# A hybrid decoder layer in fp32: the gate product as seven half-size products, after the whole output projection

## The chip, the cores and the metric

The kernel runs on one core of a Trainium2 chip. The metric is the device time of one execution in microseconds (us), as the median of repeated runs. The core has five engines that take instructions in order and wait for each other by semaphores: TensorE (PE) for matmuls, VectorE (DVE), ScalarE (ACT), GpSimd (POOL), and SyncE (SP), which issues the transfers (DMA) between the chip's memory and the core's on-chip memory SBUF. Matmul results land in PSUM, which has eight banks here; one bank holds 128x512 fp32 numbers.

## What is computed

One decoder layer on 2048 tokens of width 1024, all in fp32. Tokens are normalised and projected; 512 columns go through a state-space layer, 512 through causal differential attention with 4 heads. What comes after that is what the change touches:

```python
x = x + jnp.concatenate([y_s, y_a], axis=-1) @ w_out[i]
gate = jax.nn.sigmoid((x @ ple_w_gate[i]).astype(jnp.float32)).astype(x.dtype)
x = x + gate * (p[i] @ ple_w_proj[i])
```

`w_out` and `ple_w_gate` are 1024x1024, `ple_w_proj` is 256x1024. The last line has the PLE product, `p[i] @ ple_w_proj[i]`.

## The kernel before, in words

**Precision.** An fp32 operand is split into a high part, a cast to fp32r, and a low part, the difference of the number and its high part. A product is made in three passes (`passes`): high by high, high by low, low by high. ACT casts; DVE or POOL subtracts. Every matmul of the last phase multiplies a 128x128 weight block with 128x256 of the transposed activations, 256 tokens. So tokens come in eight units of 256, and a 1024x1024 product of one unit is 8 blocks of k by 8 of m by 3 passes, 192 matmuls; the half-size ones (512 of k, the output projection's second half) are 96, and PLE's are 48.

**Stages.** First the input projection and the state-space layer, whose result `y_s` gives the first half of the output projection, summed with the input `x` into `xp_scr` in the chip's memory beside the attention (`half`). Then attention, head by head, unit by unit; in the last head units come in the order 7, 6, ... 0. A query tile of 128 tokens ends in a chain of dependent steps: score transposes on PE (L1085), a copy on ACT (L1087), value matmuls into `po` (L1089), a square with its sum on ACT (L1092), three tiny steps on POOL (L1096 to L1098), DVE (L1099), one more transpose on PE (L1100), ACT's copy to `yo` (L1101), and a store to `yt_scr`, from which the projection loads its `yin`.

**The last phase (L1113 on).** `out_proj(i)` loads a unit's `xp_scr` as `x1` and its attention result (`load_y`: `yin`, `yh` cast on ACT at L911, `yl` difference on POOL at L912), makes four groups of 24 matmuls (`project`, L921), and DVE adds each group from PSUM to `x1` (L1138). The first three units (`EOP`) go into the pool `ps_f`, one PSUM bank that exists beside attention's (`pmf`); the others use `ps3`, the seven banks that attention leaves (`pm`). `split` casts `x1` (ACT, L1146) and subtracts (POOL, L1147) for the gate product. Per unit and block m of 128 columns PE then makes 24 gate matmuls (L1176) and 6 PLE matmuls (L1180) into one bank; ACT takes tanh (L1183), DVE does two fused steps (L1184, L1185), and the result is stored (L1188). The projection of a unit two ahead is laid behind each unit's gate. `resident` loads a weight 128 rows at a time into a buffer `yin`, casts it on ACT (L898) and subtracts on DVE (L899). It makes the second half of `w_out` (`wob`) at a fixed step of the last head, and in the last phase all of `w_gate` and `w_proj`.

**Order.** The program is written in one order of statements with priorities, and a scheduler lays the instructions of each engine in a fixed order before the run. It puts projection matmuls between the steps of the last attention units ("fillers" below). A pool of buffers can be opened on memory of another only when that one is done as a whole.

## Time and profile before

| | before |
|---|---|
| median of three runs | 1479.39 us (1478.57 to 1480.09) |
| the profiled execution | 1482.44 us, of which the span from first to last instruction is 1480.7 us |
| PE busy | 1414.4 us, 96% |
| DVE, ACT, POOL busy | 968.3, 747.7, 470.5 us |
| mean granted PE clock | 0.983 of full speed |

The profile is one execution; its times count from the first instruction. Busy is the time in which an engine executes. A row of the timeline gives start, duration, engine, line, and in square brackets how long the engine was idle ahead of it and what ended that. The chain of waits is followed back from the last instruction, at each step to what released it.

### The profile page before, as it was taken

The page shows a single profiled execution, that of the slowest core. Times are in us where ns is not written, and L with a number is a line of the kernel's source. Part 1 is how long each engine was busy: PE and PEld are TensorE (multiplying, and loading weights), DVE is VectorE, ACT ScalarE, POOL GpSimd, SP SyncE. Part 2 cuts the span into 40 slices and gives each one's busy share as a digit, 9 for nine tenths or more (in the row PEclk, how much of TensorE's full clock was granted, in tenths as well). Part 3 has the DMA queues.
Part 4 walks back from the last instruction along what each step waited for, and adds up shares of the span by engine and source line. Part 5 has one row for each costly group of instructions (what it writes and reads, how often), then busy time and mean ns, then how long its engine had stood idle before and what let it go on. Part 6 is the DMA issues. An engine that isn't in the chain of part 4 may idle for free. (4 is left out here: it accounts for less than half of the span.)

```text
span 1480.7 us, 27620 instructions
## 1 busy us (share of the span) xinstructions
PE 1414.4 (96%) x9794; PEld 1303.3 (88%) x9794; DVE 968.3 (65%) x2477; ACT 747.7 (50%) x1663; POOL 470.5 (32%) x654
## 2 busy tenths in 40 slices
PE   7899899999999999999899999999999899999998
PEld 7898798788798878887799999999889889999998
DVE  8578788799898956773777766777876253222222
ACT  8443345546644545552667677777686441111111
POOL 5632410043011410440354345455334512222110
PEclk9999999999999999999999999999999999999999
DMA  7439656546755387557753544544442243111101
GB/s 242 143 113 287 187 187 194 182 140 195 242 165 177 103 233 208 129 156 213 232 147 116 172 132 127 167 136 129 122 172 93 86 143 115 60 52 55 65 27 39
DMA packets 217971, 217.78 MB, mean 147 GB/s; under 512 B 62552, under 2 KB 169192, under 8 KB 216808
## 3 DMA queue, kind: packets, MB, share of 16 engines
q1 hardware_dynamic: 217832, 216.01, 47.9%
q8 instruction: 77, 1.26, 0.4%
q14 instruction: 62, 0.51, 0.1%
HBM read 145.90 MB, written 78.43 MB: 151 GB/s over the span
## 5 line engine op out<-in xcount | busy, mean ns | idle before, releaser
L822 PE MATMUL pmm<-wl,xh 128*128 128x512 f32 x512 | 202.8, 398 | 2.2 <-DVE wl L281 2.1
L822 PE MATMUL pmm<-wh,xl 128*128 128x512 f32 x512 | 202.2, 397 | 0.0
L822 PE MATMUL pmm<-wh,xh 128*128 128x512 f32 x512 | 198.3, 398 | 3.8 <-ACT wh L280 2.5
L1053 PE MATMUL pss<-ks,qd 128*128 128x512 f32 (+3 forms) x640 | 187.5, 390 | 9.8 <-DVE st L1055 4.1
L1064 ACT ACTIVATE s<-s,st 128x1024 f32<-128x1024 f32 (+4 forms) x192 | 171.5, 897 | 36.5 <-DVE st L1055 32.3
L1089 PE MATMUL po<-vt,wt 128*128 128x128 f32 x1088 | 151.1, 277 | 2.3 <-ACT yo L1101 1.5
L1089 PEld LDWEIGHTS po<-vt,wt 128*128 128x128 f32 x1088 | 142.0, 193 | 11.0 <-ACT yo L1101 2.8
L1176 PE MATMUL pm<-xh,wgl 128*128 128x256 f32 x512 | 143.3, 283 | 0.2 <-DVE wgl L899 0.2
L1176 PE MATMUL pm<-xl,wgh 128*128 128x256 f32 x512 | 142.6, 282 | 0.0
L1176 PE MATMUL pm<-xh,wgh 128*128 128x256 f32 x512 | 137.7, 283 | 2.1 <-ACT wgh L898 2.1
L1055 DVE CUSTOM_DVE_ANT_0 s<-pss,mk,st 128x512 f32<-128x512 f32 (+2 forms) x192 | 121.4, 652 | 26.5 <-PE pss L1053 25.1
L776 PE MATMUL pmm<-xh,wl 128*128 128x256 f32 x448 | 127.5, 288 | 2.9 <-DVE wl L281 2.9
L776 PE MATMUL pmm<-xl,wh 128*128 128x256 f32 x448 | 127.4, 288 | 0.0
L776 PE MATMUL pmm<-xh,wh 128*128 128x256 f32 x448 | 124.1, 291 | 3.2 <-DVE stg L786 2.6
L1184 DVE SCALAR_TENSOR_TENSOR th<-th,pm 128x256 f32<-128x256 f32 x64 | 26.8, 420 | 150.3 <-ACT th L1183 150.2
L1053 PEld LDWEIGHTS pss<-ks,qd 128*128 128x128 f32 x640 | 102.4, 193 | 20.9 <-DVE st L1055 8.7
L822 PEld LDWEIGHTS pmm<-wh,xh 128*128 128x128 f32 x512 | 97.2, 191 | 24.8 <-ACT wh L280 4.4
L822 PEld LDWEIGHTS pmm<-wl,xh 128*128 128x128 f32 x512 | 97.6, 191 | 21.4 <-DVE wl L281 3.0
L822 PEld LDWEIGHTS pmm<-wh,xl 128*128 128x128 f32 x512 | 97.7, 191 | 18.4
L1183 ACT ACTIVATE th<-pm 128x256 f32<-128x256 f32 x64 | 24.3, 384 | 169.6 <-PE pm L1180 168.7
L921 PE MATMUL pmf<-yh,woh 128*128 128x256 f32 x352 | 103.3, 294 | 4.8 <-DVE x L1138 3.5
L1147 POOL TENSOR_TENSOR xl<-x,xh 128x512 fp32r<-128x512 f32 x32 | 41.3, 1309 | 199.2 <-ACT xh L1146 104.7
(361 smaller groups left out, 4037.6 us busy)
## 6 DMA issues: line engine op xcount, KB each, us to landing
wraw<-in_w_in_dram SPq DMA_DIRECT2D x96, 256.0 KB
xraw<-in_x_t_dram SPq DMA_DIRECT2D x40, 256.0 KB
tab<-tab_scr SPq DMA_DIRECT2D x64, 136.0 KB
qd<-qh_scr SPq DMA_DIRECT2D x64, 128.0 KB
qd<-ql_scr SPq DMA_DIRECT2D x64, 128.0 KB
xr<-in_x_t_dram SPq DMA_DIRECT2D x32, 256.0 KB
yin<-yt_scr SPq DMA_DIRECT2D x16, 512.0 KB
xp_scr<-xp SPq DMA_DIRECT2D x32, 256.0 KB
```

Source lines behind the costliest of these rows:

```text
L776: T.matmul(pm, lhsT=w[b_][:, cb * 128:cb * 128 + 128], rhs=xt[a_][:, k, :], start=(k == 0 and n == 0), stop=(k == 7 and n == 2))
L822: T.matmul(pm, lhsT=xt[a_][:, k, j * 128:j * 128 + 128], rhs=w[b_], start=(k == 0 and n == 0), stop=(k == 7 and n == 2))
L921: T.matmul(pm[:, e, :], lhsT=w[k][b_][:, ms], rhs=y[a_][:, k, :], start=(k == 0 and n == 0), stop=(k == 3 and n == 2))
L1053: T.matmul(pss[:, :cl], lhsT=qd[:, e, m, tq], rhs=ks[m][:, c0:c0 + cl], start=e == 0, stop=e == 1)
L1055: V.tensor_tensor_reduce(sr[m][pi][:, o:o + cl], pss[:, :cl], mk[:, end - cl:end], scale=1.0, scalar=3.4e38 if ci == 0 else st[:, 2 * ci - ...
L1064: A.activation(sr[m][pi][:, :cl], sr[m][pi][:, :cl], AF.Exp, bias=st[:, ci + m:ci + m + 1], scale=-1.0, accum_out=st[:, 12 + 2 * pi + m:13 ...
L1089: T.matmul(po[:, 0:128], lhsT=wt[:, k, :], rhs=vt[:, kg + k, :], start=kg + k == 0, stop=kg + k == len(blocks_) - 1)
L1147: G.tensor_tensor(xl, x1[:, n0:n0 + 2], xh.bitcast(F32), op=ALU.subtract)
L1176: T.matmul(pm[:, 0], lhsT=wg[0][k][b_][:, ms], rhs=xc[k // 2][a_][:, k % 2], start=(k == 0 and n == 0), stop=(k == 7 and n == 2))
L1183: A.activation(th, pm[:, 0], AF.Tanh, scale=0.5)
L1184: V.scalar_tensor_tensor(th, th, 1.0, pm[:, 1], op0=ALU.add, op1=ALU.mult)
```

## The change

**The gate product by pairs.** Two units, a and b, are taken together, and the 2x2 blocks are halves of k (of `x1`, 512 each), halves of m, and the two units. Seven products of half size (4 blocks of k, 4 of m, 3 passes: 48 matmuls each, 256 tokens wide) take the place of eight. Their activation operands are halves of `x1` or sums of such halves (`s1`, `s2`, `s3`), made on DVE, then cast on ACT and subtracted on POOL (`operands`). Their weights are four quarters of `w_gate` and sums of these. The products are joined in PSUM-to-SBUF sums on DVE (`plus`), tanh and the two fused steps come after that, 512 columns wide.

**The phases.** All eight units go through the output projection first. The finished `x1` of six units is stored to `x1_scr` and loaded again for the gate; the last two stay. Two units, not three, are laid into attention's end. The projection's buffers and banks are then closed (`wo_ctx.close()`), and the gate opens its own: four banks for gate products, four for PLE.

**The weights.** The 56 tiles (7 products, 4 blocks of k, high and low; 128x512) are made in four steps, one behind each of the fourth to seventh units. A step first copies one element of the preceding unit's `x1` into both raw buffers (POOL), so that the loads (SP) come no earlier. The loads of `w_out` take four different slots.

```diff
-EOP = 3
+EOP = 2
...
-                    for k in range(4):
-                        wob[1](k)
+                    for k, slot in enumerate(("yin", "yl", "yin", "yh")):
+                        wob[1](k, slot)
...
+            def gate_w():
+                c1, c2 = slice(0, 512), slice(512, 1024)
+                def made(n, src, eng):
+                    hi, lo = wg[n][k]
+                    A.copy(hi, src)
+                    eng.tensor_tensor(lo, src, hi.bitcast(F32), op=ALU.subtract)
...
+                for k in range(4):
+                    r1, r2 = (pr3.tile([128, D], F32, name="wgr") for _ in range(2))
+                    for r_, k_ in ((r1, k), (r2, k + 4)):
+                        G.tensor_copy(r_[:, 0:1], last[0])
+                        nc.sync.dma_start(r_, w_gate[0][k_ * 128:k_ * 128 + 128, :])
+                    made(1, r1[:, c1], G)
+                    t1 = diff(r1[:, c2], r1[:, c1])
+                    made(5, t1, V)
+                    t2 = diff(r2[:, c2], t1)
+                    made(6, t2, V)
+                    yield
+                    made(2, r2[:, c1], G)
+                    made(4, diff(r2[:, c1], t2), V)
+                    made(7, diff(r2[:, c2], r1[:, c2]), V)
+                    made(3, r2[:, c2], G)
+                    yield
...
+            for t, i in enumerate(order):
+                x1 = px3.tile([128, 8, 256], F32, name="x1")
+                nc.sync.dma_start(x1, xp_scr[i])
+                y = load_y(pa3, i, 512, 2)
+                for n0 in range(0, 8, 2):
+                    pm = (ps_f if t < EOP else ps3).tile([128, 2, 256], F32, name="pmf" if t < EOP else "pm3")
+                    project(pm, wob[0], y, n0)
+                    V.tensor_tensor(x1[:, n0:n0 + 2], x1[:, n0:n0 + 2], pm, op=ALU.add)
+                if t < 6:
+                    nc.sync.dma_start(x1_scr[i], x1)
+                else:
+                    kept.append(x1)
+                if 3 <= t < 7:
+                    next(gw)
+                    next(gw)
+                last[0] = x1[:, 7, 0:1]
+        wo_ctx.close()
...
+        def product(n, x_):
+            banks = [ps_g.tile([128, 2, 256], F32, name="pg3") for _ in range(2)]
+            for mp in range(2):
+                for e in range(2):
+                    m = mp * 2 + e
+                    for k in range(4):
+                        for q, (a_, b_) in enumerate(passes):
+                            T.matmul(banks[mp][:, e], lhsT=wg[n][k][b_][:, m * 128:m * 128 + 128], rhs=x_[a_][:, k],
+                                     start=k == 0 and q == 0, stop=k == 3 and q == 2)
+            return banks
...
+            bk = step(1)
+            for mp in range(2):
+                A.copy(p1[:, mp * 2:mp * 2 + 2], bk[mp])
+            th = logits(step(2), p1)
+            plus(u2, step(6), p1)
+            u3 = pb3.tile([128, 4, 256], F32, name="p1")
+            plus(u3, step(7), u2)
+            gated(ia, 0, th, xa, ple(pa_, 0))
+            bk = step(5)
+            th = logits(bk, u3)
+            plus(u2, bk, u2)
+            gated(ib, 1, th, xb, ple(pb_, 1))
+            bk = step(3)
+            if j < 6:
+                nxt = [load_x1(order[j + 2])]
+            th = logits(bk, u2)
+            gated(ia, 1, th, xa, ple(pa_, 1))
...
```

Three places show what the change moves. Line numbers of the changed kernel are two higher up to the last phase. The first is PE at the end of attention, around the last transpose of `ya` (L1100 before, L1102 after). Before:

```order
L921 MATMUL pmf<-yl,woh_14304 128x256
L921 MATMUL pmf<-yh,woh_14306 128x256
L921 MATMUL pmf<-yh,wol_14307 128x256
L921 MATMUL pmf<-yl,woh_14306 128x256
L1100 MATMUL po<-ident,ya 128x128
L921 MATMUL pmf<-yh,woh_14300 128x256
L921 MATMUL pmf<-yh,wol_14301 128x256
L921 MATMUL pmf<-yl,woh_14300 128x256
L921 MATMUL pmf<-yh,woh_14302 128x256
L921 MATMUL pmf<-yh,wol_14303 128x256
```

After:

```order
L923 MATMUL pmf<-yl,woh_14312 128x256
L923 MATMUL pmf<-yh,woh_14314 128x256
L923 MATMUL pmf<-yh,wol_14315 128x256
L923 MATMUL pmf<-yl,woh_14314 128x256
L1102 MATMUL po<-ident,ya 128x128 x2
L1091 MATMUL po<-vt,wt 128x128 x5
L1102 MATMUL po<-ident,ya 128x128 x2
L1091 MATMUL po<-vt,wt 128x128 x2
L1102 MATMUL po<-ident,ya 128x128
L923 MATMUL pm_14922<-yh,woh_14308 128x256
L923 MATMUL pm_14922<-yh,wol_14309 128x256
```

Before, projection matmuls stand on both sides of the last transpose; after, the last transposes and value matmuls (L1091) follow each other, and the rest of the projection begins, in `pm`, behind the last of them.

The second is POOL from the end of attention on. `st` are the small steps of a query tile, `xl` and `pl` the low parts of the gate's and PLE's operands, `yl` that of the projection's, `wgr` the raw weight, `wg` its tiles. Before:

```order
L1147 TENSOR_TENSOR xl_14919<-x_14654,xh_14918 128x512
L1147 TENSOR_TENSOR xl_14923<-x_14654,xh_14922 128x512
L1147 TENSOR_TENSOR xl_14927<-x_14654,xh_14926 128x512
L1147 TENSOR_TENSOR xl_14931<-x_14654,xh_14930 128x512
L1147 TENSOR_TENSOR xl_15225<-x_14806,xh_15224 128x512
L1096 TENSOR_SCALAR st<-st 128x1 x2
L1147 TENSOR_TENSOR xl_15229<-x_14806,xh_15228 128x512
L1157 TENSOR_TENSOR pl<-pi,ph 128x512
L1097 TENSOR_TENSOR st<-st 128x1 x2
L1098 TENSOR_TENSOR st<-st,negh 128x1 x2
L912 TENSOR_TENSOR yl<-yin,yh 128x1024
```

After:

```order
L1098 TENSOR_SCALAR st<-st 128x1
L1099 TENSOR_TENSOR st<-st 128x1
L1100 TENSOR_TENSOR st<-st,negh 128x1
L1152 COPY wgr<-x_14914 128x1 x2
L914 TENSOR_TENSOR yl<-yin,yh 128x1024
L1142 TENSOR_TENSOR wg_14618<-wgr,wg_14617 128x512
L1142 TENSOR_TENSOR wg_14626<-wgr,wg_14625 128x512
L1142 TENSOR_TENSOR wg_14634<-wgr,wg_14633 128x512
L914 TENSOR_TENSOR yl<-yin,yh 128x1024
L1152 COPY wgr<-x_15027 128x1 x2
L1142 TENSOR_TENSOR wg_14620<-wgr,wg_14619 128x512
```

The low parts of the gate's operands are gone from attention's end, and behind it the two copies, the projection's `yl` and three low parts of a weight step take turns.

The third is PE where the gate begins. `oph` and `opl` are the high and low parts of an operand, `wg` the weight tiles, `pg` the banks. Before:

```order
L921 MATMUL pmf<-yh,wol_14307 128x256
L921 MATMUL pmf<-yl,woh_14306 128x256
L1176 MATMUL pm_14940<-xh_14918,wgh_14640 128x256
L1176 MATMUL pm_14975<-xh_14918,wgh_14640 128x256
L1176 MATMUL pm_15011<-xh_14918,wgh_14640 128x256
L1176 MATMUL pm_15046<-xh_14918,wgh_14640 128x256
L1176 MATMUL pm_15082<-xh_14918,wgh_14640 128x256
L1176 MATMUL pm_15117<-xh_14918,wgh_14640 128x256
L1176 MATMUL pm_15153<-xh_14918,wgh_14640 128x256
L1176 MATMUL pm_14940<-xh_14918,wgl_14641 128x256
L1176 MATMUL pm_14940<-xl_14919,wgh_14640 128x256
```

After:

```order
L923 MATMUL pm_15676<-yh,woh_14314 128x256
L923 MATMUL pm_15676<-yh,wol_14315 128x256
L923 MATMUL pm_15676<-yl,woh_14314 128x256
L1250 MATMUL pg_15764<-oph,wg_14617 128x256
L1250 MATMUL pg_15764<-oph,wg_14618 128x256
L1250 MATMUL pg_15765<-oph,wg_14617 128x256
L1250 MATMUL pg_15765<-oph,wg_14618 128x256
L1250 MATMUL pg_15824<-oph,wg_14625 128x256
L1250 MATMUL pg_15824<-oph,wg_14626 128x256
L1250 MATMUL pg_15825<-oph,wg_14625 128x256
L1250 MATMUL pg_15825<-oph,wg_14626 128x256
L1250 MATMUL pg_15764<-opl,wg_14617 128x256
```

Before, seven banks are begun with the first high parts before the first low weight is needed; after, eight matmuls need only high operands, and the ninth needs `opl`.

## Rows read from the trace of the kernel before

**Rows 1.** The page: busy time by engine; the last chain by line.

```profile
PE 1414.4 (96%) x9794; PEld 1303.3 (88%) x9794; DVE 968.3 (65%) x2477; ACT 747.7 (50%) x1663; POOL 470.5 (32%) x654
...
PE pm L1176 11%; PE pm L921 4%; PE pm L1180 3%; PE pmf L921 2%; DMA yin<-in_ple_w_gate_dram 1%; PE po L1089 1%; DVE wgl L899 0%; ACT wgh L898 0%; PE ptw L1085 0%; DMA yin<-in_ple_w_proj_dram 0%; DVE x L1138 0%; DMA yt_scr<-yo 0%; PE pss L1053 0%; DVE wpl L899 0%; ACT wph L898 0%
```

**Rows 2.** The chain of waits: start in us, duration in us, what ran.

```profile
1186.44 3.29 DMA yin<-in_ple_w_gate_dram
...
1192.09 5.56 DMA yin<-in_ple_w_gate_dram
...
1248.59 11.52 PE pm L921 x96
1260.11 2.83 PE pm L1176 x24
1262.94 0.71 PE pm L1180 x6
...
1288.51 11.52 PE pm L921 x96
```

**Rows 3.** Windows: length, busy time by engine (instructions), PE clock, DMA share, GB/s.

```profile
1192.00:1198.00 6.00, 4.54 (x35) 4.26 (x35) 1.29 (x2) 1.37 (x2) 0.00 (x0) 1.00 0.84 251
1198.00:1204.00 6.00, 5.22 (x31) 5.23 (x32) 2.45 (x2) 2.10 (x3) 0.00 (x0) 0.72 0.37 122
1250.00:1300.00 50.00, 50.00 (x423) 50.00 (x422) 12.81 (x24) 8.44 (x17) 11.88 (x9) 1.00 0.26 90
```

**Rows 4.** PE's timeline: the last head, attention's end, the first gate matmuls, the end.

```profile
1076.64 0.90 PE L1085 MATMUL ptw<-ident,s 128*128 128x128 f32 x3 [4.55 <-ACT wt L1087]
...
1159.63 0.38 PE L1085 MATMUL ptw<-ident,s 128*128 128x128 f32 x2
...
1178.22 0.71 PE L1089 MATMUL po<-vt,wt 128*128 128x128 f32 x4 [0.35 <-ACT yo L1101]
...
1182.59 0.39 PE L921 MATMUL pmf<-yh,woh 128*128 128x256 f32 x1 [0.67 <-DVE x L1138]
...
1198.78 1.67 PE L1176 MATMUL pm<-xh,wgh 128*128 128x256 f32 x7 [2.12 <-ACT wgh L898]
...
1476.37 0.28 PE L1180 MATMUL pm<-pl,wph 128*128 128x256 f32 x1
```

**Rows 5.** ACT's timeline: the last `w_out` cast of the wait, and attention's end.

```profile
1071.17 1.05 ACT L898 CAST woh<-yin 128x1024 fp32r<-128x1024 f32 x1 [2.29 <-DMA yin<-in_w_out_dram]
...
1178.96 0.28 ACT L1092 ACTIVATE ya<-po 128x128 f32<-128x128 f32 x1 [0.54 <-PE po L1089]
...
1181.95 0.37 ACT L1101 ACTIVATE yo<-po,subw 128x128 f32<-128x128 f32 x1 [2.62 <-PE po L1100]
```

**Rows 6.** POOL's timeline: the last `yl`, and an `xl`.

```profile
1169.84 2.41 POOL L912 TENSOR_TENSOR yl<-yin,yh 128x1024 fp32r<-128x1024 f32 x1 [1.36 <-DMA pi<-in_p_t_dram]
...
1187.13 3.27 POOL L912 TENSOR_TENSOR yl<-yin,yh 128x1024 fp32r<-128x1024 f32 x1 [6.58 <-ACT yh L911]
1217.96 2.74 POOL L1147 TENSOR_TENSOR xl<-x,xh 128x512 fp32r<-128x512 f32 x2 [27.55 <-PE pm L1176]
```

**Rows 7.** DVE's timeline: attention's end, gate weights, the first fused steps, the end.

```profile
1180.59 0.35 DVE L1099 SCALAR_TENSOR_TENSOR ya<-po,st,zg 128x128 f32<-128x128 f32 x1 [2.22 <-POOL st L1098]
...
1186.93 1.22 DVE L899 TENSOR_TENSOR wgl<-yin,wgh 128x1024 fp32r<-128x1024 f32 x1
...
1218.54 2.44 DVE L1185 SCALAR_TENSOR_TENSOR x<-th,x 128x256 f32<-128x256 f32 x2
...
1477.56 0.42 DVE L1185 SCALAR_TENSOR_TENSOR x<-th,x 128x256 f32<-128x256 f32 x1
```

**Rows 8.** Groups by line from 1150 us on: busy us, mean ns, idle before.

```profile
L1138 DVE TENSOR_TENSOR x<-x,pm 128x512 f32<-128x512 f32 x20 | 13.7, 687 | 36.5 <-PE pm L921 36.5
L1157 POOL TENSOR_TENSOR pl<-pi,ph 128x512 fp32r<-128x512 f32 x8 | 10.5, 1313 | 1.3 <-ACT ph L1156 1.3
L1146 ACT CAST xh<-x 128x512 fp32r<-128x512 f32 x32 | 19.5, 622 | 28.4 <-issue 14.3 <-DVE x L1138 12.1 <-PE pm L1176 1.6
```

More of the change, by code (lines that the diff above doesn't have):

```diff
@@ new lines, in hymba_kernel, with step @@
+        xa, xb = kept
+        order = order[6:] + order[:6]
+        for j in range(0, 8, 2):
+            ia, ib = order[j], order[j + 1]
+            if j == 0:
+                ops = operands(xa, xb)
+                ready = [next(ops), next(ops)]
+                ple_w()
+            pa_, pb_ = load_p(ia, 0), load_p(ib, 1)
+            p1, u2 = (pb3.tile([128, 4, 256], F32, name=n) for n in ("p1", "u2"))
+            def step(n):
+                bk = product(n, ready.pop(0))
+                nx = next(ops, None)
+                if nx is not None:
+                    ready.append(nx)
+                return bk
+            bk = step(1)
+            for mp in range(2):
+                A.copy(p1[:, mp * 2:mp * 2 + 2], bk[mp])
[13 more added lines that the diff above has]
+            gated(ia, 1, th, xa, ple(pa_, 1))
+            if j < 6:
+                nxt.append(load_x1(order[j + 3]))
+                ops = operands(*nxt)
+                ready.append(next(ops))
+            lb = ple(pb_, 0) if j == 6 else None
+            bk = step(4)
+            th = logits(bk, u3)
+            gated(ib, 0, th, xb, lb or ple(pb_, 0))
+            if j < 6:
+                xa, xb = nxt
```

162 lines of the change are left out of this document (92 added, 70 removed).

## The prediction

> **What bounds the kernel now.** The busy shares come first: TensorE (PE) is busy for 1414.4 of 1480.7 us, and the chain that ended last is mostly its matmuls [rows 1]. The chain of waits shows where that holds. From 1216 us it is an unbroken row of matmuls with one period of 39.92 us (1248.59 to 1288.51): 96 of the output projection in 11.52 us, 0.1200 us each, and eight times 24 of the gate and 6 of the PLE product, 28.40 us for 240, 0.1183 us each [rows 2]. In the window 1250 to 1300 PE is busy for 50.00 of 50 us, VectorE (DVE) for 12.81, ScalarE (ACT) for 8.44, GpSimd (POOL) for 11.88 [rows 3]. A matmul taken out there is time taken out.
>
> Three places are not of that kind. From 1182 to 1212 us the chain goes through the loads, casts and differences of the gate weights [rows 2]. From the matmul at 1182.59 to PE's end at 1476.65 [rows 4] lie 294.1 us; 504 matmuls of the output projection (24 and five units) by 0.1200 and 1920 others by 0.1183 are 287.6, so the late weights cost 6.5 us. At 1076 us PE idles 4.55 us, because ACT first waits 2.29 us for a load of `w_out` and then works off the exponentials queued behind that cast [rows 4, 5]. And while the last attention units run, PE is kept busy by output-projection matmuls laid between their dependent steps [rows 4].
>
> The measure: the profiled execution took 1482.44 us, its span is 1480.7, the median of the runs is 1479.39. I sum on the span and take the difference from the median. The runs agree within 1.5 us, so 0.2%, or 3 us, is about what a measurement here can tell from no change.
>
> **Matmuls.** 1536 gate matmuls become 7 products of 48 for each of 4 pairs, 1344; PLE's 384 and the output projection's 768 stay. The form is the same, 128x128 by 128x256. 192 by 0.1183 is 22.7 us, all on the path by [rows 3]. The phase behind the projection is 1728 matmuls, 204.4 us.
>
> **The weight loads of the projection.** The four loads of `w_out` now have slots of their own, where two waited for a buffer; the 2.29 us wait of ACT goes, and with it about 2 of PE's 4.55 us. Bounds 0 and 4.
>
> **Attention's end.** Only two units fill it, so 192 matmuls, not 264, stand ahead of the last transpose of `ya`, and 184 of them, not 136, ahead of the last score transposes, which ran at 1159.63 [rows 4] (the counts are those of the order of PE's instructions). These come at 1159.6 + 48 x 0.120 - 2 = 1163.4. Behind them three links run bare: value matmuls, ACT's square, three POOL steps, DVE, transpose, ACT's copy. The last link of before takes from 1178.22 to 1182.32, 4.1 us with 24 fillers in it; its unfilled steps (0.7 of matmuls, 1178.96 to 1180.94, transpose and copy 0.7) make 3.4 [rows 4, 5, 7]. 1163.4 + 0.4 + 3 x 3.4 = T, 1174. The projection's other banks are opened only when attention's are closed, so its 576 remaining matmuls start at T. Before was at 1182.6 with 264 fillers done; 72 fewer by 0.120 is 8.6, so the two are equal: the bare idle eats what the missing fillers give. Bounds of T: 1171, if the first link is ready as the transposes end, and 1179, if POOL's `yl` of 2.41 us [rows 6] stands in front of two links. Then the clock: after PE's idle 2.12 us at 1198.78 the granted clock is 0.72 in the mean of 6 us, that is at its lower level for some 3.4 of them: 1.7 us lost [rows 3, 4]. I charge 1.7 at T. The last 576 matmuls take 69.1 us.
>
> **The held-back weight steps.** Each of the four copies one element of the previous unit's `x1` into both raw buffers (POOL), loads 1 MB, and makes 14 tiles with 7 casts on ACT, 3 differences on POOL, 4 differences and 4 low parts on DVE. In POOL's order the copies stand right behind the `yl` of a later unit, and the next `yl` right behind the step's three differences; in ACT's order the `yh` cast stands behind the casts. So a step holds the next unit's operand. One period, by [rows 2, 5, 6, 8]: copies 0.4; two loads of 512 KB, 3.29 us alone and 5.56 with another in flight, together about 6.1; behind the second, casts (0.62) and DVE operations of 512 columns (half of 1.22) in turn, about 4.5; `yh` 1.05; `yl` 2.41. That is 14.5, plus 1.5 for the 1 MB store of `x1` ahead in the queue: 16 us. A unit takes 11.5. The first copy comes when the third unit's `x1` is summed, T + 12.2; the last unit's `yl` is three periods later, and its 11.5 us of matmuls follow. Against 69.1 that is a wait of 3P - 45.4: 2.6 us at P = 16, none below 15.1, 8.6 at 18. The copies themselves wait for a DVE sum; behind the first stands only the fifth unit's `yl`, needed 11 us later, and on SyncE (SP) behind the loads the sixth and seventh units' `yin`, with 20 us to spare: nothing. In exchange the late gate weights of before, 6.5 us, are gone: no gate load is waited for by a gate matmul, unless step four ends after the last unit, and by the same sum it ends 3 us earlier.
>
> **The passage to the gate.** The first operand's cast waits for the projection's last matmul, since their buffers overlay; then cast 1.05, difference 2.41 to 3.27 [rows 6], while PE has only 8 matmuls, 0.9 us, that need the high part alone. Idle 2.6 to 3.7: I take 3.4, and 1.7 for the clock as above.
>
> **The gate phase.** A pair has 432 matmuls, 51.1 us. DVE: five operand sums of 1.22, 14 sums from PSUM of 0.69, 8 times 0.69 and 0.85 (the steps of 0.42 now two in one), 28 us. POOL: 7 x 2.41 and 2 x 1.31, 20. ACT: 7 x 1.05 and 12 x 0.62, 15 [rows 5 to 8]. All lie beside PE; if that cover were gone, POOL's would cost first. The x1 that goes out and comes back, 12 MB, runs in windows whose DMA share was 0.26 [rows 3].
>
> **The end.** Before, PE's end to the span's end is 4.05 us: tanh, two DVE steps of which the last ends at 1477.98, and the store of 128 KB, 2.7 us [rows 4, 7]. Now a sum of 0.69, then 512-wide tanh 0.62, 0.69, 0.85, and a store of 256 KB, taken at the same 2.7 since it comes in one piece: 5.7 with gaps. Bounds 5 and 7.
>
> **Sum.** 1174 + 1.7 + 69.1 + 2.6 + 3.4 + 1.7 + 204.4 + 5.7 = 1462.6, 18.1 under 1480.7; from the median 1461.3. I say 1462.
>
> **A rule against the change.** Beside each other the two engines slow down in the trace: POOL's `yl` takes 3.27 us where a DVE difference runs beside it, 2.41 elsewhere, and two of DVE's L1185 take 2.44 beside POOL's `xl`, where one alone takes 0.42 [rows 6, 7]. The Trainium skill, "GPSIMD Engine Reference", section "1. Specifications", says that POOL shares SBUF interfaces with VectorE and contends with its instructions that have two SBUF inputs. The changed kernel puts just such differences on both engines in every step; by that rule every step would be a long one. The trace agrees where both ran.
>
> **Rivals,** their times taken from the median too. (A) The steps fit and the links are short: T 1171, no weight wait, 2.6 at the passage: 1455. For it: the period's parts overlap more than I let them. Against: 1.05 and 2.41 in a row on two engines are measured. (B) Contention as in the paragraph above: POOL's operations 0.86 longer; in a step `yl` and three differences of half the size give 0.9 + 1.3, P 18.2, the wait 9.2, and the passage 0.5 longer: 1468. For it speaks [rows 6]; against, DVE works only 5 us in a step. (C) The pair boundary: the second half's `x1` is 1 MB and comes through the queue of the output stores; then two sums of 1.22, cast 1.05, `opl` 2.41 to 3.27, some 6 to 7 us, while products 1 and 2 cover 11.4. If the load takes 8 instead of 4, the third product is late by 3 us and the clock falls for 1.7, three times: 14 us, 1475. Against: the windows' DMA share [rows 3]. (D) Slower: the step's period is the bound. Loads of 1 MB stand in one queue with the 1 MB store, the next `x1` and the next `y`; if all four are worked off ahead of a step, 3.5 MB at 251 GB/s [rows 3] is 14 us in place of 7.6, P 22.4, the wait 21.8, and PE's clock falls at each of three waits, 5 more: 1485. It decides from P = 21 on. For it: one queue carries everything. Against: stores of a finished unit can run while the step computes. (E) That the gate isn't made with fewer matmuls: the order has 1344, so nothing.
>
> **How the numbers follow.** My sum 0.60; A 0.13; B 0.10; C 0.10; D 0.07. The forecast's own bounds (T, P from 15 to 18, the end) are 1456 to 1468. The range 1454 to 1475 takes in A and B and leaves out D, most of C and a little above and below. Faster by over 0.2% is all of the sum, A and B and half of C, 0.88; D gives slower 0.06; the rest, 0.06, lies within.
>
> **What would show it.** Right: PE without gaps from the passage to the end, 51 us a pair; a bare stretch of some 10 us with three waits for DVE before the first `pm` of L923; the waits of L923 on POOL's `yl` small and only for the last one or two units; one gap of 3 us at the first `opl`. Wrong: L923 waiting for `yl` at every unit from the fifth (D, or B if POOL's operations are over 3 us), L1250 waiting for `opl` inside each pair (C), or PE waiting at T for more than 12 us.

## The result, and the profile after

The changed kernel takes 1462.24 us (median of 4 runs, 1459.01 to 1467.58), the kernel before 1479.74 beside it. The ratio is 0.9883, with a 95% interval of 0.9851 to 0.9916: by that ratio it is faster by 17.3 us. The forecast was 1462. The profiled execution took 1463.21 us, its span is 1461.5.

Two profiles differ by some us in code that is the same in both. The same PE instruction, the 349th of the `ptw` matmuls, starts here in the trace of before and in that of after (PE's timeline: start, duration, line, operation; in brackets the idle time ahead of it and what ended it):

```profile
1011.42 0.55 PE L1085 MATMUL ptw<-ident,s 128*128 128x128 f32 x3 [0.29 <-ACT wt L1087]
```

```profile
1008.20 0.55 PE L1087 MATMUL ptw<-ident,s 128*128 128x128 f32 x3 [0.29 <-ACT wt L1089]
...
1159.66 0.38 PE L1087 MATMUL ptw<-ident,s 128*128 128x128 f32 x2
...
1162.28 1.38 PE L1091 MATMUL po<-vt,wt 128*128 128x128 f32 x10 [1.06 <-ACT yo L1103]
1165.99 1.00 PE L1102 MATMUL po<-ident,ya 128*128 128x128 f32 x2 [2.33 <-DVE ya L1101]
...
1170.21 0.47 PE L1102 MATMUL po<-ident,ya 128*128 128x128 f32 x1 [2.06 <-DVE ya L1101]
1171.14 0.58 PE L923 MATMUL pm<-yh,woh 128*128 128x256 f32 x1 [0.46 <-ACT yo L1103]
...
1245.96 0.71 PE L1250 MATMUL pg<-oph,wg 128*128 128x256 f32 x4 [3.35 <-ACT oph L1223]
```

Up to that row PE has the same instructions in the same order in both, so I take the 3.2 us between 1011.42 and 1008.20 for no effect of the change. From here on I count from this **mark**. Before, the mark is 469.3 us from the span's end, after 453.3. The other rows of the second fence are the last score transposes (1159.66), three of the waits of attention's bare end, T (1171.14) and the first gate matmul (1245.96); the rows of before that answer to them are in [rows 4]. T is the first `pm` matmul of the projection, with 576 to go; stretches from the last transposes are counted from the second of the two.

By the page, PE's busy time fell by 22.5 us, from 1414.4 [rows 1] to this (busy time; then the chain by engine):

```profile
PE 1391.9 (95%) x9602; PEld 1278.8 (87%) x9602; DVE 1064.7 (73%) x2515; ACT 766.1 (52%) x1657; POOL 522.6 (36%) x670
...
PE 44%; DVE 19%; DMA 15%; POOL 7%; ACT 6%; issue 6%; SPq 3%; DVEq 0%; ACTq 0%; POOLq 0%
```

The chain is less PE than one would think: DVE and DMA have a large share of it since it runs through the weight steps, which PE does not wait for. That is seen in the windows (columns as in [rows 3]):

```profile
1150.00:1175.00 25.00, 19.03 (x130) 17.25 (x130) 6.13 (x17) 9.17 (x32) 9.29 (x24) 0.81 0.51 178
...
1200.00:1225.00 25.00, 25.00 (x211) 25.00 (x210) 19.70 (x20) 8.68 (x14) 14.32 (x11) 1.00 0.71 274
1246.00:1252.00 6.00, 5.96 (x35) 5.75 (x36) 5.96 (x3) 0.58 (x2) 4.45 (x2) 0.72 0.00 0
1300.00:1350.00 50.00, 50.00 (x419) 50.00 (x418) 32.04 (x35) 14.15 (x19) 21.00 (x9) 1.00 0.26 83
```

From 1200 to 1225, in the middle of the weight steps, PE is busy for 25.00 of 25 us. In the gate phase, 1300 to 1350, it is busy for 50.00 of 50, with DVE at 32.04, ACT at 14.15 and POOL at 21.00; before, the same length had DVE at 12.81 and POOL at 11.88 [rows 3]. The granted clock falls in two of these windows, to a mean of 0.81 around T and of 0.72 around the first gate matmul.

### The profile page after: what moved, and what is told of

The parts are those of the page before. It is cut to its first block, busy times and chain, and to the rows that moved or that the text cites. A ratio compares the mean times of both kernels' runs of the same rounds, so it can differ in the third digit from the quotient of the medians.

```text
span 1461.5 us, 27371 instructions
## 1 busy us (share of the span) xinstructions
PE 1391.9 (95%) x9602; PEld 1278.8 (87%) x9602; DVE 1064.7 (73%) x2515; ACT 766.1 (52%) x1657; POOL 522.6 (36%) x670
## 4 chain that ended last, share of the span: by engine, by line
PE 44%; DVE 19%; DMA 15%; POOL 7%; ACT 6%; issue 6%; SPq 3%; DVEq 0%; ACTq 0%; POOLq 0%
PE pg L1250 11%; PE po L1091 7%; PE pss L1055 6%; PE pmf L923 6%; PE pmm L823 4%; PE pl L1266 3%; PE ptw L1087 3%; DMA wraw<-in_w_in_dram 2%; POOL qst L845 2%; DMA tab_scr<-tx 2%; PE pss L706 1%; DMA wgr<-in_ple_w_gate_dram 1%; ACT s L1066 1%; DVE wgt L1146 1%; DVE zz L643 1%
## 5 line engine op out<-in xcount | busy, mean ns | idle before, releaser
L1250 PE MATMUL pg<-oph,wg 128*128 128x256 f32 x896 | 163.3, 285 | 3.3 <-ACT oph L1223 3.3
L1091 PE MATMUL po<-vt,wt 128*128 128x128 f32 x1088 | 151.5, 277 | 2.1 <-ACT yo L1103 1.8
L1091 PEld LDWEIGHTS po<-vt,wt 128*128 128x128 f32 x1088 | 142.7, 193 | 10.2 <-ACT yo L1103 3.3
L1250 PEld LDWEIGHTS pg<-oph,wg 128*128 128x128 f32 x896 | 140.8, 194 | 3.5 <-ACT oph L1223 3.5
L1250 PE MATMUL pg<-opl,wg 128*128 128x256 f32 x448 | 127.1, 285 | 0.0
L1057 DVE CUSTOM_DVE_ANT_0 s<-pss,mk 128x512 f32<-128x512 f32 (+3 forms) x128 | 78.2, 629 | 39.3 <-PE pss L1055 35.3
L1089 ACT COPY wt<-ptw 128x512 f32<-128x512 f32 (+3 forms) x160 | 80.8, 517 | 37.5 <-PE ptw L1087 32.3
L595 POOL TENSOR_TENSOR U<-U,rl 128x256 f32<-128x256 f32 x32 | 30.4, 951 | 186.4 <-DMA U<-ug_scr 145.9
L923 PE MATMUL pmf<-yh,woh 128*128 128x256 f32 x320 | 93.6, 293 | 1.7 <-ACT xp L979 1.4
```

The source lines that it names most:

```text
L595: UE.tensor_tensor(U, U, rl, op=ALU.mult)
L923: T.matmul(pm[:, e, :], lhsT=w[k][b_][:, ms], rhs=y[a_][:, k, :], start=(k == 0 and n == 0), stop=(k == 3 and n == 2))
L1057: V.tensor_tensor_reduce(sr[m][pi][:, o:o + cl], pss[:, :cl], mk[:, end - cl:end], scale=1.0, scalar=3.4e38 if ci == 0 else st[:, 2 * ci - ...
L1089: A.copy(wt[:, :nk], ptw[:, :nk])
L1091: T.matmul(po[:, 0:128], lhsT=wt[:, k, :], rhs=vt[:, kg + k, :], start=kg + k == 0, stop=kg + k == len(blocks_) - 1)
L1250: T.matmul(banks[mp][:, e], lhsT=wg[n][k][b_][:, m * 128:m * 128 + 128], rhs=x_[a_][:, k], start=k == 0 and q == 0, stop=k == 3 and q == 2)
```

## What the runs showed

Times of before that are given with a run were measured beside it on the same chip. The theory that the prediction left: the 192 matmuls are the gain, the steps are hidden but for 3 us, and small terms (T, passage, slots) make up the rest. The rivals: the steps' period sets the end, or contention of POOL and DVE does.

**1. The changed kernel again.** No edit; it is the control for the others.

> The changed kernel itself, unaltered, once more. If the passage to the gate is held by VectorE's queue (the low parts of the last weight step, then the last unit's four sums), a second profile shows the same gap of about 3.3 us with the sums ending at the gap's end; if the second operand's low part on GpSimd holds it, PE starts its first 8 gate matmuls earlier and stops behind them. The time should be 1459 to 1466 us; a wait for yl in the last unit, whose margin in the first profile was 1.4 us, would show as 1465 and more.

1459.38 us, 0.9874 (0.9845 to 0.9904). From the mark to the end 449.9 us, where the first profile has 453.3; of the 3.3, 2.5 lie between the mark and T. A single profile is good to 2 or 3 us there and no better. The passage is the same: PE idles 3.22 us ahead of the first gate matmul, for 3.35 in the first profile.

**2. The old buffers of `w_out`,** all four loads in slot `yin`:

```diff
-                    for k, slot in enumerate(("yin", "yl", "yin", "yh")):
+                    for k, slot in enumerate(("yin", "yin", "yin", "yin")):
```

> The changed kernel with the four w_out loads back in one kind of buffer (two slots in turn). Theory: the slots of their own take away PE's idle 4.55 us at 1076 us and the lower clock behind it, 3.4 us in the window 1075 to 1100, so this kernel is 3 to 6 us slower, 1465 to 1468. Rival: the scheduler lays 48 more projection matmuls into the bare end of attention when the weights come later, so the loss comes back there: within 1.5 us of the changed kernel.

1456.92 us, 0.9856 (0.9823 to 0.9889): not slower, in the median 2.5 us faster than run 1, which the intervals do not separate. PE's timeline:

```profile
1071.50 0.90 PE L1087 MATMUL ptw<-ident,s 128*128 128x128 f32 x3 [3.40 <-ACT wt L1089]
...
1166.28 0.38 PE L923 MATMUL pm<-yh,woh 128*128 128x256 f32 x1 [1.17 <-ACT yo L1103]
```

The wait for `w_out` is back, 3.40 us at 1071.50. But the projection's weights are ready later, so the order puts more of its matmuls behind the last score transposes: 56 between them and T, where the changed kernel has 8. From the last transposes to T is 11.58 us here and 11.37 in both profiles of the changed kernel. 48 matmuls, 5.8 us, went into that chain for nothing, and at T only 1.17 us of idle are left. The 576 matmuls behind T then take 69.25 us, at full clock, against 71.35 and 70.73. To remove the wait saves 3.4 us, and costs 5.8 of cover and 1.5 to 2.1 of clock.

**3. The new buffers alone, in the kernel before:**

```diff
-        def load(k):
+        def load(k, slot="yin"):
...
-            raw = raws.tile([128, 4, 256], F32, name="yin").rearrange("q a b -> q (a b)")
+            raw = raws.tile([128, 4, 256], F32, name=slot).rearrange("q a b -> q (a b)")
...
-                    for k in range(4):
-                        wob[1](k)
+                    for k, slot in enumerate(("yin", "yl", "yin", "yh")):
+                        wob[1](k, slot)
```

> The kernel before with only the four different slots for the w_out loads. Theory: the idle of 4.55 us and the clock behind it go, 3 to 4 us faster than before, 1476. Rival: the last head is bound elsewhere and the time comes back by attention's end: within 1 us of 1479.5.

1483.5 us, 1.0024 (1.0010 to 1.0038) of before: slower by 3.6. The 4.55 us of idle at 1076 [rows 4] are gone, but 56 matmuls have left the end of the chain: 96 lie behind the last score transposes, where before has 152. The last link is bare, and behind the last transpose of `ya` the gate begins at once, before its weights are there. PE's waits from 1174 us through the first gate matmuls add up to 8.4 us here and to 3.9 in before, where the longest is the 2.12 at 1198.78 [rows 4]. Three of them:

```profile
1179.72 0.71 PE L1089 MATMUL po<-vt,wt 128*128 128x128 f32 x4 [1.06 <-ACT yo L1101]
...
1183.37 0.47 PE L1100 MATMUL po<-ident,ya 128*128 128x128 f32 x1 [2.94 <-DVE ya L1099]
...
1187.44 1.86 PE L1176 MATMUL pm<-xh,wgh 128*128 128x256 f32 x7 [3.60 <-ACT wgh L898]
```

The first two, 4.0 us, are attention's. The third, with 0.8 us of smaller ones behind it, is for gate weights: 4.4 us, where before waits 2.3. Runs 2 and 3 agree, one from each side: this part of the change gained nothing.

**4. Three units at attention's end,** as in the kernel before: `EOP = 2` becomes `EOP = 3`.

> The changed kernel with three units, not two, laid into attention's end. Theory: the bare end of attention, some 6 us of PE idle from 1162 to 1171 us and 2.4 us of lower clock in the first unit behind it, is filled with 72 matmuls that then need not follow: 7 to 10 us faster than the changed kernel, 1453 to 1455, if the weight steps keep up with one unit less to hide beside. Rival: the steps, three periods of 13.4 to 16.3 us, then set the end: the last unit waits for yl or the first gate matmul for step four, and 3 us or less are gained, 1459 to 1462.

1459.17 us, 0.9871 (0.9839 to 0.9902), as run 1. 72 more matmuls, 8.64 us, lie between the last transposes and T, and that stretch grows by only 3.5, to 14.9. But PE now waits for a `yl`:

```profile
1224.14 0.38 PE L923 MATMUL pm<-yl,woh 128*128 128x256 f32 x1 [2.27 <-POOL yl L914]
```

The first copies stand at 1178.75 here and the last `yl` ends 45.3 us after them; PE gets to it after 43.1 us, where the changed kernel has 45.4 between the same two. So cover for the bare chain and cover for the weight steps come out of one stock of matmuls. By the profiles this run is 3.1 and 6.4 us shorter from the mark (446.9) than the two of the changed kernel; in the medians the choice of two or three units makes no difference that shows.

**5. Product 7 made twice,** both halves of its columns, which is eight products' work, 192 matmuls more:

```diff
-            for mp in range(2):
+            for mp in list(range(2)) * (2 if n == 7 else 1):
```

> The changed kernel with product 7 made twice over into the same banks, so eight half-size products a pair as a plain product would need; 192 matmuls more, nothing else. If the gate phase is bound by PE alone, it takes 192 x 0.120 = 23.0 us more, 1483 to 1486, and the seventh product is worth what the count says. Rival: the sums on VectorE and the low parts on GpSimd hide some of the scheme's gain, then the extra matmuls are partly covered and the price is 10 to 18 us.

1484.3 us, 1.0044 (1.0028 to 1.0060) of the kernel before. From the first gate matmul to PE's end is 232.12 us, against 209.36 and 209.27: 22.8 for 192, 0.119 each. The chain shows the stretch of four products, which was of 192 matmuls and 23.04 us, now of 240:

```profile
1307.15 28.80 PE pg L1250 x240
```

The gate phase is PE's, and the saved product is worth its matmuls. It also shows the price of all else: without the saved product the changed kernel is 6.9 us slower than before, though the late gate weights, 6.5 us in the trace of before, are gone.

**6. The weight steps one unit earlier:** `if 3 <= t < 7` becomes `if 2 <= t < 6`.

> The changed kernel with the four weight steps placed one unit earlier. In the profiles the passage's gap of 3.3 us ends when VectorE has made the last unit's four sums, which stood behind the last low parts of step four. Theory: with these low parts out of the way the sums end 0.7 us behind PE's last matmul, PE starts its 8 first gate matmuls about 1.3 us after it (a cast of 1.05 us), and then waits for GpSimd's opl, 1 to 1.7 us: the gap splits in two, 2.5 to 3 us in all, a gain of 0.5 to 1 us. Rival: the cast of the operand is what holds PE, then the gap stays 3.3 us. A cost on the other side: the first copies stand in attention's end; if they hold yl or the small steps there, T comes later.

1463.71 us, 0.9907 (0.9874 to 0.9939): no gain. PE's passage to the gate changes its form, though:

```profile
1247.86 0.74 PE L1250 MATMUL pg<-oph,wg 128*128 128x256 f32 x4 [1.26 <-ACT oph L1223]
...
1248.81 0.74 PE L1250 MATMUL pg<-oph,wg 128*128 128x256 f32 x4 [0.21 <-ACT oph L1223]
...
1250.74 0.38 PE L1250 MATMUL pg<-opl,wg 128*128 128x256 f32 x1 [1.19 <-POOL opl L1224]
```

One wait of 3.35, put down to `oph`, has become three, of 1.26, 0.21 and 1.19, for `oph`, the next `oph` and `opl`. What had been last in the passage was therefore something that the fourth step delays. That is DVE, as these two fences of the changed kernel show (first DVE's timeline, then ACT's):

```profile
1227.36 2.89 DVE L1146 TENSOR_TENSOR wgt<-wgr 128x512 f32<-128x512 f32 x1
...
1241.58 1.88 DVE L1142 TENSOR_TENSOR wg<-wgt,wg 128x512 fp32r<-128x512 f32 x3
1243.38 2.47 DVE L1176 TENSOR_TENSOR x<-x,pm 128x512 f32<-128x512 f32 x4
```

```profile
1243.63 1.99 ACT L1223 CAST oph<-x 128x1024 fp32r<-128x1024 f32 x2 [1.91 <-DVE wg L1142]
```

The fourth step's three low parts (L1142, 1241.58 to 1243.46) stand in DVE's order ahead of the last four sums of the projection (L1176, 1243.38 to 1245.85). The sums read the banks that the first gate product is to be written to, and PE starts at 1245.96, 0.11 us behind them. The `oph` that the row names doesn't fit: its cast, the first of the two, took 1.04 and was done at 1244.67. In run 1 the sums end at 1240.78 and PE starts at 1240.88; in runs 2, 4, 5, 8 and 10 the distance is 0.10 or 0.11 too, and in this run, whose last low parts are made earlier, it is 0.53, and PE starts 0.05 us behind the first cast. In run 4 even the second cast ends after PE has started.

**7. The steps delayed:** each copy becomes a difference that fills its whole buffer, 128x1024, not one column.

```diff
-                        G.tensor_copy(r_[:, 0:1], last[0])
+                        G.tensor_tensor(r_, last[0], last[0], op=ALU.subtract)
...
-                last[0] = x1[:, 7, 0:1]
+                last[0] = x1[:, 4:8].rearrange("q a b -> q (a b)")
```

> The changed kernel with each one-element copy made a GpSimd operation of the whole raw buffer (about 2.4 us each, two a step), everything else alike. The steps' period grows by 4.8 us from the measured 16.3, 14.8 and 13.4. By the prediction's formula the last unit's yl comes three periods after the first copy: 3 x 4.8 + 4.8 of the first copies, less the 1.4 us of margin, so PE waits 13 to 18 us and the kernel is that much slower, 1473 to 1478, with the clock's fall on top. Rival: the period isn't a chain through GpSimd but set by the loads or by PE's pace (the yh cast waits for PE), so that most of the 4.8 is absorbed: under 6 us slower.

1467.8 us, 0.9938 (0.9912 to 0.9964): 5.6 over the changed kernel and 8.4 over run 1, and not the 13 to 18 that the formula seemed to ask for. From the mark the run is 9.5 us longer than the mean of the two profiles. POOL's timeline, then one row of DVE and one of PE:

```profile
1182.69 3.75 POOL L1152 TENSOR_TENSOR wgr<-x 128x1024 f32<-128x1024 f32 x2 [15.60 <-DVE x L1176]
...
1199.20 4.51 POOL L1152 TENSOR_TENSOR wgr<-x 128x1024 f32<-128x1024 f32 x2 [1.29 <-DVE x L1176]
...
1217.06 4.51 POOL L1152 TENSOR_TENSOR wgr<-x 128x1024 f32<-128x1024 f32 x2 [0.69 <-DVE wgt L1146]
1221.53 2.86 POOL L914 TENSOR_TENSOR yl<-yin,yh 128x1024 fp32r<-128x1024 f32 x1
1224.34 5.17 POOL L1142 TENSOR_TENSOR wg<-wgr,wg 128x512 fp32r<-128x512 f32 x3
1230.81 4.51 POOL L1152 TENSOR_TENSOR wgr<-x 128x1024 f32<-128x1024 f32 x2 [1.29 <-DVE wgt L1146]
```

```profile
1248.27 1.27 DVE L1176 TENSOR_TENSOR x<-x,pm 128x512 f32<-128x512 f32 x2
```

```profile
1249.65 2.14 PE L1250 MATMUL pg<-oph,wg 128*128 128x256 f32 x8 [10.16 <-ACT oph L1223]
```

The periods became 16.5, 17.9 and 13.8 us, where these rows of the changed kernel's POOL give 16.3, 14.8 and 13.4:

```profile
1185.80 0.30 POOL L1152 COPY wgr<-x 128x1 f32<-128x1 f32 x2 [16.03 <-DVE x L1176]
...
1202.14 1.26 POOL L1152 COPY wgr<-x 128x1 f32<-128x1 f32 x2
...
1216.97 0.64 POOL L1152 COPY wgr<-x 128x1 f32<-128x1 f32 x2 [0.67 <-POOL yl L914]
1222.18 4.71 POOL L1142 TENSOR_TENSOR wg<-wgr,wg 128x512 fp32r<-128x512 f32 x3 [4.57 <-ACT wg L1141]
1226.84 2.85 POOL L914 TENSOR_TENSOR yl<-yin,yh 128x1024 fp32r<-128x1024 f32 x1
1230.38 1.12 POOL L1152 COPY wgr<-x 128x1 f32<-128x1 f32 x2 [0.68 <-DVE wgt L1146]
```

POOL's order is not the same in the two kernels. In the changed kernel the last `yl` (1226.84) stands behind the third step's differences (1222.18). Here it stands ahead of them (1221.53 and 1224.34), right behind the third copies: two periods after the first copies and not three. So PE waits for no `yl`, and this run does not test the prediction's formula.

What it tests is the fourth step. PE idles 10.16 us at the passage, 6.8 more than in the first profile, and behind that the granted clock is 0.50 in the mean of 6 us, which makes the gate phase 2.7 us longer; the two are the 9.5. PE starts 0.11 behind DVE's last sums (1248.27 and 1.27), and 0.09 behind the first operand's cast, which ends with them here. The steps' period does come to the end of the projection, by the fourth step and DVE's order, not by `yl`. The long differences on POOL also run beside DVE's, so part of the delay may be contention; the run doesn't separate the two.

**8. The gate phase's operands moved by 96 bytes:** an unused tile of 24 columns ahead of their pool.

```diff
+        pad3 = p3.enter_context(tc.tile_pool(name="p3pad", bufs=1))
+        pad3.tile([128, 24], F32, name="pad3")
         pop = p3.enter_context(tc.tile_pool(name="p3o", bufs=3))
```

> The changed kernel with 96 bytes left empty in front of the operand buffers of the gate, so that the moving operands begin at the same offset in 128 bytes as in the kernel before. Theory: the interval of the gate's matmuls, exactly 0.1200 us in the changed kernel and 0.1183 in the mean before, depends on where the operands lie; then it falls to about 0.1183 and the gate phase is 3 us shorter. Rival: it hangs on something else (weights, banks, order), and the interval stays 0.1200.

1463.92 us, 0.9908 (0.9879 to 0.9937). The interval of the gate's matmuls stays at 0.120 us in the mean: 192 in 23.03, where before 240 took 28.40, 0.1183 each [rows 2]. So this offset doesn't bring the shorter mean back. It does change the single intervals: by the starts on PE's timeline, those between gate matmuls from 1262 to 1440 us are 0.119 to 0.121 us in the changed kernel, 0.115 to 0.125 here and 0.115 to 0.127 before. The operands' place has a part in the pattern, no other place was tried, and why the mean grew stays open.

**9. No hold-back:** the line with POOL's copy is taken out, and the steps' loads start when their buffers are free.

```diff
-                        G.tensor_copy(r_[:, 0:1], last[0])
```

> The changed kernel without the one-element copies that hold the loads of the gate weights back; the loads then wait for their two raw buffers alone. Theory: nothing of the steps is on the path except the end of step four, whose low parts and the sums behind them hold PE at the passage; with the loads earlier the steps end earlier, the sums keep up with PE, and the gap at the passage splits as in the run with the steps one unit earlier, 2.7 us for 3.3: within 1.5 us of the changed kernel. Rival: the loads, 8 times 512 KB, then collide with attention's own transfers and VectorE takes up the differences in front of attention's last links: T comes 2 us or more later and the kernel is slower by that.

1461.87 us, 0.9886 (0.9855 to 0.9917): the same as the changed kernel. Waits moved (the passage is 1.18, 0.22 and 1.26 as in run 6; the last link of attention's end idles 3.50 in place of 2.06), and the sum stayed. The copies neither cost nor gave what can be measured.

**10. The projection's `yl` on DVE:**

```diff
-        G.tensor_tensor(yl, raw, yh.bitcast(F32), op=ALU.subtract)
+        (V if r0 else G).tensor_tensor(yl, raw, yh.bitcast(F32), op=ALU.subtract)
```

> The changed kernel with the last phase's yl made on VectorE (about 1.2 us) in place of GpSimd (2.4). In the profiles a VectorE difference of 512 columns, 0.68 us alone, takes 2.89 us where it runs into yl on GpSimd, and yl itself 2.85. Theory of the shared interface: these rows of 2.9 us vanish, a step loses about 2 us, step four ends 2 to 5 us earlier against the first matmul of the projection's rest, and the gap at the passage falls from 3.3 us to 2.7 or less. Rival: the long rows are waits for data that only look like contention; then they stay. The order at attention's end also shifts, so the time as a whole may move by 2 us either way.

1453.7 us, 0.9833 (0.9798 to 0.9867): 8.2 under run 9 on the same chip, the best of all. It was made against the contention that this row of the changed kernel's DVE shows, printed above: a difference of 512 columns that takes 2.89 us at 1227.36, beside POOL's `yl` from 1226.84 to 1229.69, and 0.68 alone. DVE's timeline here, the third step and the last sums:

```profile
1197.05 0.69 DVE L1146 TENSOR_TENSOR wgt<-wgr 128x512 f32<-128x512 f32 x1 [2.69 <-DMA wgr<-in_ple_w_gate_dram]
...
1204.70 1.21 DVE L914 TENSOR_TENSOR yl<-yin,yh 128x1024 fp32r<-128x1024 f32 x1
...
1232.29 2.47 DVE L1176 TENSOR_TENSOR x<-x,pm 128x512 f32<-128x512 f32 x4
```

`yl` takes 1.21 on DVE, where POOL needs 2.41 to 2.85, and no difference of 2.89 is left in the steps; the longest of L1146 is 1.79. But most of the gain lies elsewhere. PE's timeline, from the last score transposes through T to the gate:

```profile
1152.65 0.38 PE L1087 MATMUL ptw<-ident,s 128*128 128x128 f32 x2
...
1163.53 0.39 PE L923 MATMUL pm<-yh,woh 128*128 128x256 f32 x1 [1.28 <-ACT yo L1103]
...
1234.86 1.18 PE L1250 MATMUL pg<-oph,wg 128*128 128x256 f32 x8 [1.95 <-ACT oph L1223]
...
1236.55 0.39 PE L1250 MATMUL pg<-opl,wg 128*128 128x256 f32 x1 [0.51 <-POOL opl L1224]
```

From the mark T comes after 154.3 us, not 162.9 or 160.4: the order now has 48 matmuls behind the last transposes and has no wait for `w_out` either, the two things that runs 2 and 3 could have only one at a time. The idle ahead of T is 1.28 us, and the 576 matmuls take 69.26. T and the clock are 6.2 to 8.7 and 1.5 to 2.1 of the 8.4 to 11.8 us by which the run is shorter from the mark. That the shorter `yl` is why the order came out so, and not its mere move to another engine, was not told apart.

**11. A version from the findings,** without the move of `yl`: the edits of runs 2 and 6, the first gate operand made during the projection in a free `x1` buffer, and the last block finished in four pieces of 256 columns.

```diff
+            f = px3.tile([128, 8, 256], F32, name="x1")
+            first = (f[:, 0:4].bitcast(F32R), f[:, 4:8].bitcast(F32R))
+            A.copy(first[0], kept[0][:, 0:4])
+            G.tensor_tensor(first[1], kept[0][:, 0:4], f[:, 0:4], op=ALU.subtract)
...
-            yield made(xi_[:, K1])
+            yield first or made(xi_[:, K1])
...
+            if j == 6:
...
+                for m in range(4):
+                    t_, b_ = th[:, m], bk[m // 2][:, m % 2]
+                    V.tensor_tensor(t_, b_, u3[:, m], op=ALU.add)
+                    A.activation(t_, t_, AF.Tanh, scale=0.5)
...
+                    nc.sync.dma_start(out[ib][:, m:m + 1], th[:, m:m + 1])
```

> The changed kernel with what the runs point to: the w_out loads in their old slots (the bare end of attention filled with 48 matmuls), the weight steps one unit earlier, the first operand's two parts made during the last unit in the third x1 buffer, and the last block's sums, tanh and stores in four pieces of 256 columns. Theory: 2.5 us from the slots, the passage from 3.3 us and the clock behind it to about 1 us (PE's last matmul, the last sum 0.7, semaphores), 2.3 plus up to 1.7; the end from 6.2 to 4.5 us: 1452 to 1454 where the changed kernel is at 1460 to 1462. Rival: the earlier steps cost attention's end what the passage gains, as the run with early steps alone (1463.7) may say: 1456 to 1458.

1458.08 us, 0.9866 (0.9834 to 0.9898): nothing over run 1. The parts did what they were for. The passage is 0.82 us, the gate phase takes 207.59 in place of 209.3 since the clock does not fall, the end 5.54 in place of 6.15. But the last `yl` is now late (PE's timeline, then POOL's):

```profile
1228.15 0.39 PE L923 MATMUL pm<-yl,woh 128*128 128x256 f32 x1 [3.06 <-POOL yl L914]
...
1241.99 2.27 PE L1254 MATMUL pg<-x,wg 128*128 128x256 f32 x17 [0.82 <-issue]
```

```profile
1225.30 2.79 POOL L914 TENSOR_TENSOR yl<-yin,yh 128x1024 fp32r<-128x1024 f32 x1
```

The steps stand one unit earlier in POOL's order, so the last `yl` comes behind one more of them. Run 6 has that order too and no such wait: there the first copies stood 10.4 us ahead of T, here 0.5. PE waits 3.06 us, the granted clock is 0.72 over the 6 us from 1228.15 on, and the projection takes 74.82 us, where run 2 had 69.25. What the passage and the end gave back was lost a unit earlier.

**12. The parts of run 11, except the old buffers, on top of run 10.**

> The kernel with yl on VectorE, and with it the weight steps one unit earlier, the first operand made during the last unit, and the last block in four pieces (the w_out loads as in the changed kernel). Theory: the passage falls from 2.0 + 0.5 us of waits to about 0.9 as in the run with these three and the old slots, and the end by 0.6; the last unit's yl no longer waits behind GpSimd's differences, so the 3.3 us that PE lost there with the earlier steps do not come back: 2 to 3 us under the run with yl on VectorE alone (1453.7), 1451. Rival: yl stands behind the last step's loads on VectorE just as it did on GpSimd, PE waits 1 to 4 us in the last unit, and nothing is gained, 1453 to 1455.

1454.03 us, 0.9831 (0.9808 to 0.9854): the same as run 10, for the same reason as in run 11, though `yl` is on DVE:

```profile
1213.38 0.39 PE L923 MATMUL pm<-yl,woh 128*128 128x256 f32 x1 [0.94 <-DVE yl L914]
...
1227.01 0.39 PE L923 MATMUL pm<-yl,woh 128*128 128x256 f32 x1 [1.85 <-DVE yl L914]
...
1240.85 1.43 PE L1254 MATMUL pg<-x,wg 128*128 128x256 f32 x10 [0.83 <-issue]
```

Two waits for `yl`, 0.94 and 1.85, in exchange for a passage of 0.83.

## Where the prediction was right, and where only its sum was

Its terms from the common mark, in us; before's mark is 1011.42, so T at 1174 is 162.6 from it (the passage counts from the end of the projection's last interval, 0.1 us more than PE's idle):

| term | forecast | profile after | run 1 |
|---|---|---|---|
| mark to T | 162.6 | 162.9 | 160.4 |
| 576 matmuls, clock at T | 70.8 | 71.4 | 70.7 |
| wait for the steps | 2.6 | 0 | 0 |
| passage | 3.4 | 3.5 | 3.3 |
| gate phase, clock there | 206.1 | 209.4 | 209.3 |
| end | 5.7 | 6.1 | 6.2 |
| sum | 451.2 | 453.3 | 449.9 |

**The matmuls** were right in kind: run 5 gives 22.8 us for 192. The chain of the changed kernel shows the phase without gaps (start, duration, what):

```profile
1171.14 13.88 PE pm L923 x96
...
1299.81 23.04 PE pg L1250 x192
...
1351.64 23.04 PE pg L1250 x192
```

Each matmul was mis-sized: 192 in 23.04 is 0.1200, and I had taken 0.1183 over from [rows 2]. 1728 times the difference is 2.9 us, the largest error of the sum. The same row group showed 0.1200 for the projection's matmuls of the same shape, so 204.4 to 207.4 was a bound that I should have kept.

**Attention's end** came out in size: the last transposes at 151.6 and 149.1 from the mark, for 152.0, and 11.4 us from there to T for 10.6. Its make-up was another. Not three bare links of 3.4 lie there, but 2.5 us to the first value matmuls (1162.28) and 8.9 in two rounds from there to T, the first with two query tiles side by side (`x2` at 1165.99). And I had the missing 72 fillers as neither gain nor loss, each of them costing the chain its full time, 8.6 us in all. Run 4 measured 3.5 us for the 72; of the 5.1 that they then give, 2.3 goes to a wait, and the medians show none of the rest.

**The slots** failed as a term. I took off 2 us for ACT's wait and did not ask what an earlier weight does to the order: runs 2 and 3 show that it pulls 48 and 56 fillers out of the chain. The net is between nothing and a loss of 3.6.

**The weight steps.** Nothing was waited for, where I had 2.6 us. The formula's path was right: in the changed kernel the last `yl` ends three periods behind the first copies, 43.9 us from 1185.80. That is 14.6 a period where I had 16, and by the formula there is no wait below 15.1. So the period was the term that was mis-sized. Up to the end of POOL's differences the three steps took 11.8, 11.3 and 9.9 us, for 12.5 in the sum, of which no row showed the 1.5 for the store; and in the second and third the `yh` cast no longer stood between the differences and `yl` (1222.18 and 1226.84). The last `yl` ends at 1229.69, and the last unit's first matmul that needs it is this one of PE:

```profile
1231.17 0.28 PE L923 MATMUL pm<-yl,woh 128*128 128x256 f32 x1
```

So 1.5 us are to spare. I had also written that the fourth step ends 3 us ahead of the last unit and costs nothing. By the sum's own terms (copies 0.4, loads 6.1, work 4.5, against 11.5 us of matmuls) it was 0.5, and less than nothing with the store. It ended at 1243.46, about 1 us behind the projection, and it costs at the passage: DVE's last low parts stand ahead of the last sums.

**The passage** was right by size, 3.4, and wrong by cause. I had the first operand's cast and POOL's `opl` as the last; in the changed kernel `opl` is never waited for, and DVE's sums come last. In runs 6 and 9, where the sums are early, the links that I had named appear, with 2.66 us in three pieces. So this is two waits of about the same length, one behind the other's back.

**The rivals.** Contention (B) is there and is hidden in the changed kernel: DVE operations of 2.89, 2.43 and 3.28 beside POOL, where they take 0.68 and 1.22 alone, and PE still has no wait in the steps. C, the pair boundary, did not come: in the chain a pair's first 192 matmuls start at 1299.81 and the next pair's at 1351.64, 51.83 us later, and 432 matmuls by 0.1200 are 51.84. D would have had PE wait at each unit; it waits at none. A had the right picture for the steps and the wrong price for the gate.

That the forecast held by 0.2 us is luck. Errors cancelled: 2.9 for the gate's interval, 0.6 for the clock at T and 0.4 for the end against 2.6 for a wait that did not come. Even so the sum from the mark is 2.1 us under the first profile and 1.3 over that of run 1, and the median of the same kernel was 1459.38 the second time. The spread of its range was made of the size of T and of the steps; the largest error, the gate's interval, was in neither.

## What to carry to other kernels

Price the work that a change leaves in place, too, at the largest duration that its shape shows anywhere in the trace, and keep the smaller as the other bound. A load that comes earlier is not a gain by itself where work is laid out by readiness: it may take the fillers out of the one chain that needs them, so look at what stands in that chain's gaps afterwards. When a wait's named releaser had ended well ahead, look for the instruction that ended a tenth of a us before the waiter starts, and try it by moving that one; and before moving background work earlier to free the end of a stage, count what it will then stand in front of. An edit that is meant to delay one engine can change the order that the scheduler lays down, as in run 7; compare the order before you read the time.

## What was not expected of the hardware

**DVE and POOL take turns.** A DVE difference of 128x512 that overlaps a POOL difference takes not a little longer but POOL's time: it starts at 1227.36, POOL's `yl` ends at 1229.69, and it ends 0.56 us later, at 1230.25; alone it takes 0.68. DVE's sums with a PSUM bank as one input kept their 0.67. The Trainium skill, "SBUF — State Buffer", section "SBUF: two separate sides", calls the port pair of the two an exclusive lock, held for a whole instruction, taken by a DVE operation with two SBUF inputs or by POOL, and says that the other fully blocks. The rows agree.

**The matmuls' interval.** The gate's matmuls, 128x128 by 128x256, came every 0.1183 us in the mean before and every 0.1200 in the changed kernel, at a granted clock of 1.00. Another offset of the operands scattered the single intervals and left the mean so (run 8). Its cause is open.

**What a short idle costs.** Behind the idle of 3.35 us at the passage the granted clock was 0.72 over 6 us, some 1.7 us lost at the lower level of 1.2 GHz; behind one of 0.82 in run 11 it stayed at 1.00, and the phase was shorter by 1.8 us. The length of the idle does not settle it alone: with waits of 1.26, 0.21 and 1.19 us in run 6 the granted clock stayed at 1.00 from 1247.8 to 1253.8, and with waits of 1.18, 0.22 and 1.26 in run 9 it was 0.82 from 1245 to 1251 and 0.89 over the 6 us behind that. At T, with 2.06 and 0.46 us of idle just ahead, the first 96 matmuls took 13.88 us in the chain above, where 96 take 11.52 [rows 2].
